# Seven-product feed-forward loop: products grown in two PSUM chains, partial sums copied out by ScalarE

## The chip, the cores and the metric

One core of a Trainium2 chip runs the whole network in one launch. The metric is device time in microseconds (us). Engines: TensorE (PE; its weight loads are PEld), VectorE (DVE), ScalarE (ACT), GpSimd (POOL) and SyncE (SP), which issues most DMAs. TensorE writes to PSUM, which has eight banks; VectorE and ScalarE read it.

## The reference

Two layers with Macaron feed-forward blocks over 512 latent and 256 context tokens, width 1024, hidden width 2816, all in float32. A feed-forward block is

```
def swiglu(h, w_in, w_out):
    a, b = jnp.split(h @ w_in, 2, axis=-1)
    return (jax.nn.silu(a) * b) @ w_out

def ffn_substep(x, mods, w_in, w_out, g, b):
    shift, scale, gate = mods
    y = swiglu(modulate(x, shift, scale), w_in, w_out)
    return layer_norm(ALPHA * x + MACARON * gate * y, g, b)
```

It stands four times in the program, twice in each layer: FF1 and FF2 around the even mixer of layer 0, FF3 and FF4 around the odd one of layer 1. FF1 to FF3 work on 768 tokens, FF4 on the 512 latent ones. The modulation (`mods`) of each substep is a product of the conditions with `w_ada`.

## The kernel before

Features lie on partitions. Every float32 operand is split into a high and a low float32r part: ScalarE casts the high part (line 115), VectorE subtracts it for the low part (line 117), and a product is three matmuls, high by high, high by low, low by high (`mm3`, lines 154 to 156).

The hidden layer (`ffn`) has 22 blocks of 128 hidden units, each with gate weights (A1 = A11, A12) and value weights (A2 = A21, A22). The first 3 blocks (5 in FF4) are plain products. The other 19 (17) go through `seven`: the 2 x 2 products over halves of features and halves of tokens (384 columns each, 256 in FF4) are made of seven products in Winograd's form, each 4 steps of three matmuls, 84 matmuls in a block. They are named here in the order in which TensorE runs them: P1 = A11 B11, P2 = A12 B21, P3 = S2 T2, P4 = S1 T1, P5 = S3 T3, P6 = S4 B22, P7 = A22 T4. T1 to T4 are made once (tiles `six` and `xh`), S1 to S4 for each block. In the text a prime marks what belongs to the next block.

Around one block x, other engines do this:

- GpSimd makes the next blocks' S1, S2, S3 from freshly loaded weights (lines 645, 646, 647: **sum 1, sum 2, sum 3**; `ahead`) and S4' (line 654).
- ScalarE and VectorE split A1', S12', A2' and S4' (tiles `r4h`, `r4l`, `r4s`, eight buffers, seven used in a block). A1' has the number of its raw weights in its name; S12' is read from `late`, S4' goes to `r4s`.
- Raw weights come by DMA into four buffers `raw`, two in a block; the second load for block x+2 waits until S4 of block x is split.
- Each product has a PSUM bank of its own out of seven (`ps`, tag h). P1 is copied out by ScalarE (line 670), and VectorE adds the others to copies in SBUF: seven additions a block (line 668). Two silu run on ScalarE (672, 679). `put` multiplies gate and value (556, 560); what belongs to the second half of the tokens goes to DRAM.
- In FF1 and FF2 the **modulation** of later substeps runs beside the first 13 of the 19 blocks (`ada`): 24 loads of `w_ada`, for each one VectorE product with running sum for the latent tokens (line 183) and one for the context tokens, which by turns is a second one on VectorE, or a product on GpSimd (line 186) that ScalarE then sums (line 187). FF3 has 16 such loads, latent only; FF4 has none.

Each engine runs its instructions in one order, which a scheduler fixes when the program is built. Names in the rows end in a buffer's number.

Of the kernel before, what the change touches and what calls it, by code (L numbers as in the profile page):

```python
# [14 lines left out]
AF = mybir.ActivationFunctionType  # L15
# [3 lines left out]
P = 128  # L19
D = 1024  # L20
# [21 lines left out]
class Net:  # L42
# [70 lines left out]
    def split(self, h, l, src, lo="vector"):  # L113
        """src = h + l, each in float32r"""
        self.copied = self.nc.scalar.copy(out=h, in_=src)  # L115
        eng = self.nc.vector if lo == "vector" else self.nc.gpsimd
        eng.tensor_sub(out=l, in0=src, in1=h.bitcast(F32))  # L117

    def weights(self, dram, lo="vector", spare=None):
        """spare: a pool with room for them beside the stream's"""  # L120
# [10 lines left out]
    def behind_weights(self):  # L131
        """for loads and copies that would else be queued before those of the last weights"""
        st = ExitStack()
        for i in self.fetched:
            st.enter_context(self.tc.issue_after(i.ins))
        return st

    def late(self):
        """for what a phase leaves to the next: the second half's norm works there"""
# [11 lines left out]
    def mm3(self, ps, h, l, xh, xl, first, last):  # L151
        """first, last: of the products that go to the bank, in which two sums may lie"""
        mm = self.nc.tensor.matmul
# [5 lines left out]
    def load_c(self, tiles):  # L159
        """silu of the conditions in every partition; the first call leaves it in DRAM for the later ones"""  # L160
# [38 lines left out]
    def ada(self, sections, tiles, room, steps):  # L199
        """the modulation's sections, (layer, section), in so many steps; tiles for the conditions, room() for weights: [P, D]"""  # L200
# [24 lines left out]
    def start(self, pool):  # L225
        """The first modulation, half of the features after the other; yields before the first block and after each.
        The modulation's columns are made on the tensor engine, which has nothing else to do yet."""
# [47 lines left out]
    def affine(self, l, i, nxt):  # L275
        """columns of the norm's affine and, with the next modulation folded in, of the next input"""
# [68 lines left out]
    def rsqrt(self, a, eps_tile, eps, y, t):  # L345
        """y = 1/sqrt(a + eps): exp(-ln/2), then one step of Newton"""
# [9 lines left out]
    def table(self, name, after):  # L356
        """a function table ahead of its use; the one with both exp and ln the scheduler would else fetch apart"""
# [4 lines left out]
    def out_phase(self, pool, nk, wsrc, gsplit, halves, gate, l, i, nxt, r_of, table=None, keep=False, ada=iter(())):  # L362
        """y^T = w^T g over nk blocks; gsplit(kk, c0, c1) -> (hi, lo) of blocks 2kk, 2kk+1;
        wsrc(q, kk) -> [P, 1024] of blocks 2kk, 2kk+1 and the features' half q"""
# [11 lines left out]
        def operands(step):  # L376
            """the second pass loads the weights again, and ahead to where the first half's operand was,
            unless there is room to keep them"""
# [66 lines left out]
    def add_up(self, s, r, j):  # L445
        """the blocks' sum in two parts, of the even and the odd"""
# [19 lines left out]
    def settle(self, steps=None):  # L466
        """what is left of the norm of the second half: its first steps, or all"""
# [4 lines left out]
    def project(self, ws, halves, ps_of, done, group, early=None, spare=None, after=None):  # L472
        """ws: list of weight APs; ps_of(u, h) -> PSUM AP for half h (None: both in one), done(u, h) once it is there.
        The first `group` weights go half by half, and the second half of the input may come late;
        with `early`, which makes the input, they go block by block."""
# [54 lines left out]
    def ffn(self, l, p, halves, nxt, ada=((), ()), table=None, first_of_all=False):  # L530
        """ada: what else is to be made of the conditions while the hidden layer's two products go on"""
# [6 lines left out]
        with ExitStack() as st:  # L538
# [13 lines left out]
            def put(x, a, b, gate, up):  # L552
                """the hidden layer's block x, tokens a..b; the first half's stay on chip"""
# [11 lines left out]
            def r_of(h, j):  # L565
                """sums of the output product and the residual; the first half's later blocks lie where G was"""
# [13 lines left out]
            def ps_of(u, h):  # L580
                """a narrow half's gate and value share a bank"""
# [23 lines left out]
            # tokens in two halves of m, as in the seven products of Strassen and Winograd  # L605
# [5 lines left out]
            def sums_of_inputs():  # L611
                """T2 = B22 - T1, T3 = B22 - B12, T4 = B21 - T2 of T1 = B12 - B11"""
# [23 lines left out]
            def ahead(x, sums):  # L636
                """block x of the gate's weights, A11 and A12, and of the value's, A21 and A22: the sums but one,
                S1 = A21 + A22, S2 = S1 - A11, S3 = A11 - A21 (in A21's place)"""
# [11 lines left out]
            def seven(x, raw, sums):  # L650
# [10 lines left out]
                def product(w, b):  # L661
                    ps = self.ps()[:, :m]
                    for k in range(4):
                        ks = slice(k * P, (k + 1) * P)
                        self.mm3(ps, w[0][:, ks], w[1][:, ks], b[0][:, k, :], b[1][:, k, :], k == 0, k == 3)
                    return ps

                add = lambda o, a, b: nc.vector.tensor_add(out=o, in0=a, in1=b)  # L668
                u2, c11, u4, c22 = (self.tmp("c")[:, :m] for _ in range(4))
                nc.scalar.copy(out=u2, in_=product(part(A1, 0), B(0, 0)))  # L670
                add(c11, u2, product(part(A1, 1), B(1, 0)))
                nc.scalar.activation(out=c11, in_=c11, func=AF.Silu)
                add(u2, u2, product(part(S12, 1), made[2]))
# [646 lines left out]
```

## Time and profile before

| | us |
|---|---|
| median of 3 runs (lowest to highest) | 2876.92 (2876.66 to 2877.67) |
| span of the profiled execution | 2874.1 |
| TensorE busy | 2685.2 (93%) |
| VectorE busy | 2185.1 (76%) |
| ScalarE busy | 1237.0 (43%) |
| GpSimd busy | 1074.6 (37%) |

The profiled execution has no time of its own beside its span; the median is 2.8 us above it, which is what lies around the span. Busy shares are means over stages with different limits; the loop of each feed-forward block has to be read by itself.

### The profile page before, as it was taken

The page shows a single profiled execution, that of the slowest core. Times are in us where ns is not written, and L with a number is a line of the kernel's source. Part 1 is how long each engine was busy: PE and PEld are TensorE (multiplying, and loading weights), DVE is VectorE, ACT ScalarE, POOL GpSimd, SP SyncE. Part 2 cuts the span into 40 slices and gives each one's busy share as a digit, 9 for nine tenths or more (in the row PEclk, how much of TensorE's full clock was granted, in tenths as well). Part 3 has the DMA queues.
Part 4 walks back from the last instruction along what each step waited for, and adds up shares of the span by engine and source line. Part 5 has one row for each costly group of instructions (what it writes and reads, how often), then busy time and mean ns, then how long its engine had stood idle before and what let it go on. Part 6 is the DMA issues. An engine that isn't in the chain of part 4 may idle for free.

```text
span 2874.1 us, 44394 instructions
## 1 busy us (share of the span) xinstructions
PE 2685.2 (93%) x17168; PEld 2449.1 (85%) x17168; DVE 2185.1 (76%) x3131; ACT 1237.0 (43%) x1919; POOL 1074.6 (37%) x762
## 2 busy tenths in 40 slices
PE   7889999999999888999999899999999998999997
PEld 4789998887877778989788899998987777999997
DVE  3999978765774689997977888664745887778856
ACT  2333333544543343333345433332534667544444
POOL 0655522241220465643334644410424332366402
PEclk9999999999999999999999999999999999999998
DMA  5343255542114223334555333254541101423454
GB/s 221 111 147 112 105 174 207 195 152 67 56 37 152 88 96 139 118 119 139 206 200 180 110 134 119 82 189 165 184 149 59 41 34 45 158 92 122 155 192 157
DMA packets 139671, 374.24 MB, mean 130 GB/s; under 512 B 16962, under 2 KB 48066, under 8 KB 139460
## 3 DMA queue, kind: packets, MB, share of 16 engines
q1 hardware_dynamic: 136832, 370.21, 37.3%
q8 instruction: 135, 2.21, 0.3%
q10 hardware_dynamic: 2628, 1.20, 0.2%
q14 instruction: 76, 0.62, 0.1%
HBM read 337.78 MB, written 33.56 MB: 129 GB/s over the span
## 4 chain that ended last, share of the span: by engine, by line
PE 58%; DVE 22%; issue 7%; ACT 5%; POOL 4%; DMA 3%; SPq 0%; DVEq 0%; POOLq 0%; ACTq 0%
PE ps L156 17%; PE ps L154 17%; PE ps L155 17%; DVE r4l L117 3%; DVE trash L183 3%; DVE c L668 2%; DVE spare L556 1%; DMA raw<-in_w_ffn_out 1%; PE ps L1187 1%; PE ps L1188 1%; PE ps L1189 1%; DVE sm L1089 1%; DVE b L621 1%; ACT r4h L115 1%; DVE late_g L560 1%
## 5 line engine op out<-in xcount | busy, mean ns | idle before, releaser
L117 DVE TENSOR_TENSOR r4l<-raw,r4h 128x1024 fp32r<-128x1024 f32 (+1 forms) x350 | 449.5, 1286 | 215.5 <-ACT r4h L115 176.3
L154 PE MATMUL ps<-xh,r4h 128*128 128x384 f32 (+2 forms) x1672 | 562.5, 337 | 16.6 <-ACT xh L115 7.0
L155 PE MATMUL ps<-xl,r4h 128*128 128x384 f32 (+2 forms) x1672 | 559.1, 335 | 4.8 <-DVE xl L117 3.2
L156 PE MATMUL ps<-xh,r4l 128*128 128x384 f32 (+2 forms) x1672 | 559.0, 335 | 0.0
L115 ACT CAST r4h<-raw 128x1024 fp32r<-128x1024 f32 (+1 forms) x366 | 358.7, 982 | 443.2 <-PE ps L155 330.7
L156 PE MATMUL ps<-six,r4l 128*128 128x384 f32 (+1 forms) x888 | 294.7, 332 | 69.5 <-DVE r4l L117 69.5
L154 PEld LDWEIGHTS ps<-xh,r4h 128*128 128x128 f32 x1672 | 315.1, 189 | 39.7 <-ACT xh L115 9.5
L155 PEld LDWEIGHTS ps<-xl,r4h 128*128 128x128 f32 x1672 | 315.4, 189 | 24.8 <-DVE xl L117 4.9
L156 PEld LDWEIGHTS ps<-xh,r4l 128*128 128x128 f32 x1672 | 315.4, 189 | 18.1
L668 DVE TENSOR_TENSOR c<-c,ps 128x384 f32<-128x384 f32 (+1 forms) x518 | 261.8, 518 | 49.4 <-PE ps L156 39.5
L154 PE MATMUL ps<-six,r4h 128*128 128x384 f32 (+1 forms) x888 | 292.6, 330 | 0.0
L155 PE MATMUL ps<-six,r4h 128*128 128x384 f32 (+1 forms) x888 | 291.4, 328 | 0.0
L156 PE MATMUL ps<-r4h,r4l 128*128 128x512 f32 (+1 forms) x768 | 278.5, 363 | 13.7 <-DVE r4l L117 13.7
L154 PE MATMUL ps<-r4h 128*128 128x512 f32 (+1 forms) x768 | 278.6, 363 | 0.0
L155 PE MATMUL ps<-r4l,r4h 128*128 128x512 f32 (+1 forms) x768 | 277.3, 361 | 0.0
L156 PE MATMUL ps<-r4h,spare 128*128 128x256 f32 (+1 forms) x896 | 261.0, 292 | 11.5 <-DVE spare L117 11.5
L154 PE MATMUL ps<-r4h,spare 128*128 128x256 f32 (+1 forms) x896 | 263.6, 294 | 1.5 <-ACT spare L115 1.5
L155 PE MATMUL ps<-r4l,spare 128*128 128x256 f32 (+1 forms) x896 | 260.6, 291 | 0.1
L156 PEld LDWEIGHTS ps<-six,r4l 128*128 128x128 f32 x888 | 170.8, 192 | 77.6 <-DVE r4l L117 77.6
L645 POOL TENSOR_TENSOR late<-raw 128x512 f32<-128x512 f32 x74 | 116.6, 1575 | 255.1 <-DMA raw<-in_w_ffn_in 219.2
L654 POOL TENSOR_TENSOR raw<-raw,late 128x512 f32<-128x512 f32 x74 | 98.2, 1327 | 251.3 <-DVE r4l L117 233.8
L156 PEld LDWEIGHTS ps<-r4h,spare 128*128 128x128 f32 x896 | 172.8, 193 | 16.3 <-DVE spare L117 14.2
(292 smaller groups left out, 5969.8 us busy)
## 6 DMA issues: line engine op xcount, KB each, us to landing
raw<-in_w_ffn_in SPq DMA_DIRECT2D x176, 512.0 KB, 4.0
raw<-in_w_ffn_out SPq DMA_DIRECT2D x176, 512.0 KB, 4.2
spare<-in_w_ada SPq DMA_DIRECT2D x80, 512.0 KB, 5.0
six<-in_w_ada SPq DMA_DIRECT2D x64, 512.0 KB, 5.3
g<-late_g SPq DMA_DIRECT2D x88, 128.0 KB, 2.2
raw<-g SPq DMA_DIRECT2D x44, 256.0 KB, 3.3
raw<-in_w_in_even SPq DMA_DIRECT2D x20, 512.0 KB, 3.4
raw<-in_w_in_odd SPq DMA_DIRECT2D x16, 512.0 KB, 3.3
```

Of the source, the lines that this page charges most:

```text
L115: self.copied = self.nc.scalar.copy(out=h, in_=src)
L117: eng.tensor_sub(out=l, in0=src, in1=h.bitcast(F32))
L154: mm(out=ps, lhsT=h, rhs=xh, start=first, stop=False)
L155: mm(out=ps, lhsT=h, rhs=xl, start=False, stop=False)
L156: mm(out=ps, lhsT=l, rhs=xh, start=False, stop=last)
L183: nc.vector.scalar_tensor_tensor(out=self.tmp("trash").bitcast(BF16), in0=r, scalar=1.0, in1=self.c_bc[v], op0=ALU.mult, op1=ALU.mult, acc ...
L556: nc.vector.tensor_mul(out=G(x)[:, 0, a:e], in0=gate[:, :e - a], in1=up[:, :e - a])
L560: nc.vector.tensor_mul(out=t, in0=gate[:, o:b - a], in1=up[:, o:b - a])
L621: sub = lambda o, a, b: nc.vector.tensor_sub(out=o, in0=a, in1=b)
L645: nc.gpsimd.tensor_add(out=s1, in0=a21, in1=a22)
L654: nc.gpsimd.tensor_sub(out=a12, in0=a12, in1=sums[:, 512:])
L668: add = lambda o, a, b: nc.vector.tensor_add(out=o, in0=a, in1=b)
```

## The change

In `seven` the products no longer have a bank each. X takes P1, then P3, P5 and P7 on top; Y takes P4, then P6. P2 keeps its own. Sums on the way are read between two products of a chain: ScalarE copies X after P1 (u1) and after P3 (u2), and Y after P4 (p5); VectorE adds P2 to u1, X after P5 to p5, and Y after P6 to u2. X after P7 goes straight into `put`. The flag `chain` only tells the builder that a bank is read inside a group. (The diff also drops comments, so lines move by one to ten.)

```
-                def product(w, b):
-                    ps = self.ps()[:, :m]
+                def grow(ps, w, b):
+                    first = ps is None
+                    ps = self.ps()[:, :m] if first else ps
                     for k in range(4):
                         ks = slice(k * P, (k + 1) * P)
-                        self.mm3(ps, w[0][:, ks], w[1][:, ks], b[0][:, k, :], b[1][:, k, :], k == 0, k == 3)
+                        self.mm3(ps, w[0][:, ks], w[1][:, ks], b[0][:, k, :], b[1][:, k, :], first and k == 0, k == 3,
+                                 True)
                     return ps
 
                 add = lambda o, a, b: nc.vector.tensor_add(out=o, in0=a, in1=b)
-                u2, c11, u4, c22 = (self.tmp("c")[:, :m] for _ in range(4))
-                nc.scalar.copy(out=u2, in_=product(part(A1, 0), B(0, 0)))
-                add(c11, u2, product(part(A1, 1), B(1, 0)))
-                nc.scalar.activation(out=c11, in_=c11, func=AF.Silu)
-                add(u2, u2, product(part(S12, 1), made[2]))
-                add(u4, u2, product(part(S12, 0), made[1]))
-                p7 = product(part(A2, 0), made[3])
-                add(c22, u4, p7)
-                add(u2, u2, p7)
-                add(u4, u4, product(S4, B(1, 1)))
-                nc.scalar.activation(out=u4, in_=u4, func=AF.Silu)
-                add(u2, u2, product(part(A2, 1), made[4]))
-                put(x, 0, m, c11, u2)
-                put(x, m, n, u4, c22)
+                copy = lambda o, a: nc.scalar.copy(out=o, in_=a)
+                u1, u2, p5 = (self.tmp("c")[:, :m] for _ in range(3))
+                X = grow(None, part(A1, 0), B(0, 0))
+                copy(u1, X)
+                add(u1, u1, grow(None, part(A1, 1), B(1, 0)))
+                nc.scalar.activation(out=u1, in_=u1, func=AF.Silu)
+                grow(X, part(S12, 1), made[2])
+                copy(u2, X)
+                Y = grow(None, part(S12, 0), made[1])
+                copy(p5, Y)
+                grow(X, part(A2, 0), made[3])
+                add(p5, p5, X)
+                grow(Y, S4, B(1, 1))
+                add(u2, u2, Y)
+                nc.scalar.activation(out=u2, in_=u2, func=AF.Silu)
+                grow(X, part(A2, 1), made[4])
+                put(x, 0, m, u1, X)
+                put(x, m, n, u2, p5)
```

TensorE's instructions stand in the same order as before. On the other engines the order moves in all four loops. ScalarE, late in FF1's modulation, before (one block's tail and the next one's head; `spare` with `mod` is the sum of line 187):

```order
L679 ACTIVATE c_1751<-c_1751 128x384
L670 COPY c_1895<-ps_1899 128x384
L115 CAST r4s_1892<-raw_1726 128x512
L187 ACTIVATE spare_1720,mod_0_1_102<-spare_1720 128x1024
L115 CAST r4h_2026<-raw_1872 128x1024
L672 ACTIVATE c_1896<-c_1896 128x384
L115 CAST r4h_2030<-late_528 128x1024
```

And now, about the same place (c_1840 is u2, c_1841 p5, c_1979 the next block's u1):

```order
L675 COPY c_1840<-ps_1842 128x384
L675 COPY c_1841<-ps_1884 128x384
L116 CAST r4h_1972<-raw_1818 128x1024
L689 ACTIVATE c_1840<-c_1840 128x384
L189 ACTIVATE spare_1810,mod_0_1_102<-spare_1810 128x1024
L116 CAST r4s_1976<-raw_1816 128x512
L116 CAST r4h_2102<-raw_1956 128x1024
L675 COPY c_1979<-ps_1982 128x384
```

The modulation's sum stood behind the copy of P1 and the cast of S4'; now it stands ahead of both casts and of the copy. In the blocks before these (the second to the seventh of the loop) it stands one place further up, ahead of the second silu. VectorE at this place, before, from the additions of P5 on (`trash` is the modulation's product, r4l_1889 the low part of A2'):

```order
L668 TENSOR_TENSOR c_1752<-c_1751,ps_1810 128x384
L668 TENSOR_TENSOR c_1749<-c_1749,ps_1810 128x384
L183 SCALAR_TENSOR_TENSOR trash_1862,mod_0_0_101<-spare_1581,spare_697 128x1024
L668 TENSOR_TENSOR c_1751<-c_1751,ps_1825 128x384
L183 SCALAR_TENSOR_TENSOR trash_1864,mod_0_1_102<-spare_1581,spare_698 128x1024
L556 TENSOR_TENSOR spare_1854<-c_1751,c_1752 128x128
L560 TENSOR_TENSOR late_g_1857<-c_1751,c_1752 128x256
L668 TENSOR_TENSOR c_1749<-c_1749,ps_1840 128x384
L183 SCALAR_TENSOR_TENSOR trash_1868,mod_0_0_101<-spare_1720,spare_697 128x1024
L556 TENSOR_TENSOR spare_1854<-c_1750,c_1749 128x384
L117 TENSOR_TENSOR r4l_1889<-raw_1728,r4h_1888 128x1024
L117 TENSOR_TENSOR r4s_1892<-raw_1726,r4s_1892 128x512
```

And now, from the low part of A1' on:

```order
L118 TENSOR_TENSOR r4l_1964<-raw_1816,r4h_1963 128x1024
L674 TENSOR_TENSOR c_1839<-c_1839,ps_1856 128x384
L118 TENSOR_TENSOR r4l_1968<-late_528,r4h_1967 128x1024
L185 SCALAR_TENSOR_TENSOR trash_1944,mod_0_0_101<-spare_1804,spare_697 128x1024
L674 TENSOR_TENSOR c_1841<-c_1841,ps_1842 128x384
L185 SCALAR_TENSOR_TENSOR trash_1946,mod_0_1_102<-spare_1804,spare_698 128x1024
L195 TENSOR_TENSOR mod_0_0_101<-mod_0_0_101,bada_86 128x8
L185 SCALAR_TENSOR_TENSOR trash_1952,mod_0_0_101<-spare_1810,spare_697 128x1024
L674 TENSOR_TENSOR c_1840<-c_1840,ps_1884 128x384
```

One modulation product now stands between the low part of S12' and the addition for which P7 waits (c_1841). The product on `spare_1810`, on which GpSimd's product and then ScalarE's sum hang, is the third of the block.

## Rows read from the trace of the kernel before

**Rows 1.** The page of the whole execution: its span, and part 1 (busy time, share of the span, instructions, by engine; PEld is TensorE's weight loads).

```profile
span 2874.1 us, 44394 instructions
PE 2685.2 (93%) x17168; PEld 2449.1 (85%) x17168; DVE 2185.1 (76%) x3131; ACT 1237.0 (43%) x1919; POOL 1074.6 (37%) x762
```

**Rows 2.** Busy time of each engine in six stretches of the seven-product loops: FF1 while the modulation runs beside it, and after; FF2 likewise; FF3; FF4. Columns: stretch and its length, then busy us and number of instructions of TensorE, its weight loads, VectorE, ScalarE and GpSimd, granted clock, DMA share, GB/s.

```profile
106.00:302.40 196.40, 177.95 (x979) 174.78 (x978) 192.55 (x234) 71.92 (x108) 103.92 (x56) 0.98 0.38 134
302.40:410.00 107.60, 106.06 (x597) 104.79 (x596) 84.48 (x124) 38.21 (x53) 42.91 (x26) 1.00 0.35 117
1057.00:1252.00 195.00, 178.24 (x976) 174.84 (x976) 191.37 (x234) 69.86 (x106) 104.26 (x56) 0.98 0.38 135
1252.00:1361.00 109.00, 107.08 (x602) 105.73 (x601) 87.28 (x127) 38.08 (x53) 43.66 (x26) 1.00 0.34 117
1643.60:1910.00 266.40, 266.40 (x1511) 265.97 (x1510) 201.37 (x289) 92.67 (x125) 109.41 (x68) 1.00 0.35 119
2565.90:2727.00 161.10, 161.10 (x1347) 161.10 (x1347) 141.97 (x211) 76.60 (x112) 88.05 (x57) 1.00 0.40 134
```

**Rows 3.** The copy of the first product (line 670, one in each hidden block) in each of the four loops: count, ns min/median/max, start of the first and of the last one.

```profile
L670 ACT COPY c<-ps x19: 458/467/480, 106.0 to 395.8; 128x384 f32<-128x384 f32 x19
L670 ACT COPY c<-ps x19: 457/462/479, 1057.0 to 1346.3; 128x384 f32<-128x384 f32 x19
L670 ACT COPY c<-ps x19: 469/479/481, 1631.3 to 1895.2; 128x384 f32<-128x384 f32 x19
L670 ACT COPY c<-ps x17: 361/373/374, 2553.2 to 2716.9; 128x256 f32<-128x256 f32 x17
```

**Rows 4.** What TensorE waited for in FF1's loop (106 to 410 us, first row) and in FF2's (1057 to 1361 us): us in total, times, longest.

```profile
PE ps L156 <- DVE r4l L117: 19.2, 11, 2.9
PE ps L156 <- DVE r4l L117: 17.8, 11, 2.9
```

**Rows 5.** Lines 668, 117, 183, 186 and 654 in FF1's loop beside the modulation (106 to 302.4 us): count, ns min/median/max, start of the first and last, shape.

```profile
L668 DVE TENSOR_TENSOR c<-c,ps x82: 539/546/556, 109.0 to 302.0; 128x384 f32<-128x384 f32 x82
L117 DVE TENSOR_TENSOR r4l<-raw,r4h x24: 1211/1215/3414, 107.3 to 297.2; 128x1024 fp32r<-128x1024 f32 x24
L117 DVE TENSOR_TENSOR r4s<-raw,r4s x12: 677/680/2879, 108.4 to 296.1; 128x512 fp32r<-128x512 f32 x12
L117 DVE TENSOR_TENSOR r4l<-late,r4h x12: 1225/1764/2141, 112.3 to 298.8; 128x1024 fp32r<-128x1024 f32 x12
L183 DVE SCALAR_TENSOR_TENSOR trash<-spare x31: 1212/1835/3225, 114.4 to 291.1; 128x1024 bf16<-128x1024 f32 x31
L183 DVE DVE_READ_ACCUMULATOR trash<-spare x31: 76/77/84, 115.5 to 292.2; 128x1 f32 x31
L186 POOL TENSOR_TENSOR spare<-spare x11: 2391/2583/3383, 115.7 to 292.4; 128x1024 f32<-128x1024 f32 x11
L654 POOL TENSOR_TENSOR raw<-raw,late x12: 1283/1292/1317, 110.8 to 298.6; 128x512 f32<-128x512 f32 x12
```

**Rows 6.** The timeline of GpSimd and VectorE in FF1 (start and length in us; the wait ahead of it in brackets): one place where they meet.

```profile
239.61 2.62 POOL L186 TENSOR_TENSOR spare<-spare 128x1024 f32<-128x1024 f32 x1 [3.32 <-DVE trash L183]
239.93 3.38 DVE L117 TENSOR_TENSOR r4l<-raw,r4h 128x1024 fp32r<-128x1024 f32 x1
```

**Rows 7.** ScalarE's timeline in FF1 (columns as above).

```profile
236.44 0.62 ACT L115 CAST r4s<-raw 128x512 fp32r<-128x512 f32 x1
242.26 1.06 ACT L187 ACTIVATE spare<-spare 128x1024 f32<-128x1024 f32 x1 [5.20 <-POOL spare L186]
243.22 0.18 ACT L187 ACTIVATION_READ_ACCUMULATOR spare<-spare 128x1 f32 x1
243.32 1.03 ACT L115 CAST r4h<-raw 128x1024 fp32r<-128x1024 f32 x1
244.41 0.52 ACT L672 ACTIVATE c<-c 128x384 f32<-128x384 f32 x1
```

**Rows 8.** The timeline of one hidden block of FF3: the first matmul of the third, the fifth and the seventh product, VectorE's two subtractions (rows in order of engine, not of time).

```profile
1749.07 0.34 PE L154 MATMUL ps<-six,r4h 128*128 128x384 f32 x1
1753.30 0.34 PE L154 MATMUL ps<-six,r4h 128*128 128x384 f32 x1
1757.52 0.34 PE L154 MATMUL ps<-six,r4h 128*128 128x384 f32 x1
1749.15 1.23 DVE L117 TENSOR_TENSOR r4l<-raw,r4h 128x1024 fp32r<-128x1024 f32 x1 [1.26 <-issue]
1753.39 1.23 DVE L117 TENSOR_TENSOR r4l<-late,r4h 128x1024 fp32r<-128x1024 f32 x1 [1.46 <-PE ps L155]
```

**Rows 9.** One weight load of FF1: the subtraction that frees its buffer, its issue on SyncE's queue, and GpSimd's first sum from it.

```profile
226.89 0.69 DVE L117 TENSOR_TENSOR r4s<-raw,r4s 128x512 fp32r<-128x512 f32 x1 [1.39 <-ACT r4s L115]
227.61 0.33 SPq L642 DMA_DIRECT2D raw<-in_w_ffn_in  x1
230.94 1.74 POOL L645 TENSOR_TENSOR late<-raw 128x512 f32<-128x512 f32 x1 [0.49 <-DMA raw<-in_w_ffn_in]
```

**Rows 10.** Busy time and granted clock in two stretches of FF1 (columns as in rows 2).

```profile
240.00:243.40 3.40, 0.83 (x6) 0.51 (x4) 3.40 (x3) 1.14 (x3) 2.23 (x1) 1.00 0.74 263
243.60:246.90 3.30, 3.30 (x11) 3.30 (x11) 3.29 (x5) 3.15 (x4) 1.15 (x1) 0.50 0.76 232
```

**Rows 11.** Line 668 in FF4's loop (columns as in rows 5).

```profile
L668 DVE TENSOR_TENSOR c<-c,ps x112: 405/415/423, 2568.4 to 2725.5; 128x256 f32<-128x256 f32 x112
```

More of the change, by code (lines that the diff above doesn't have):

```diff
@@ L1 @@
+import functools
 import itertools
@@ L149, in ps, with mm3 @@
         return self.psum.tile([P, 512], F32, tag=tag, name="ps", bufs=self.psum_bufs[tag])
-    def mm3(self, ps, h, l, xh, xl, first, last):
-        mm = self.nc.tensor.matmul
+    def mm3(self, ps, h, l, xh, xl, first, last, chain=False):
+        mm = functools.partial(self.nc.tensor.matmul, skip_group_check=chain)
         mm(out=ps, lhsT=h, rhs=xh, start=first, stop=False)
```

## Prediction

> **What bounds the kernel now.** I read the page first, then the loops one by one. TensorE is busy 93% of the span, no other engine over 76% [rows 1], so only a stage in which TensorE waits can give anything. The stretches show where it does in the loops that change: in FF3 and FF4 it is busy for the whole stretch, 266.4 of 266.4 us and 161.1 of 161.1, while in FF1 and FF2, as long as the modulation runs beside them, it lacks 18.5 and 16.8 us, and after that less than 2 [rows 2]. A block at full pace takes 14.79 us: four products lie between 1749.07 and 1757.52, 2.113 us each, times seven [rows 8]. From the first copy to the last, 18 blocks, FF1 takes 289.8 us and FF2 289.3 [rows 3], against 266.2 at full pace: they lose 23.6 and 23.1 us, **46.7 in all, the most that the change can win in the loops**. What TensorE waits for there is, 11 times in each loop and up to 2.9 us, a low part of weights from VectorE [rows 4]. VectorE is busy for 192.6 of those 196.4 us [rows 2]. The first 13 blocks bear the loss, so a block there takes about 14.79 + 23.4/13 = 16.6 us.
>
> That VectorE is full does not mean that it works all the time. An addition from PSUM takes 0.54 to 0.56 us throughout; a subtraction of two SBUF operands takes 1.21 us at best and up to 3.41 [rows 5]. One such stands beside GpSimd's product: it starts at 239.93, the product ends at 242.23, the subtraction at 243.31, 1.08 later [rows 6]. The two take turns.
>
> The Trainium skill has this as a rule ("SBUF — State Buffer", section "Who interferes with whom"): a VectorE instruction with two SBUF inputs and a GpSimd instruction that reads SBUF exclude each other for a whole instruction; one with a single SBUF input goes free. The rows agree [rows 5, 6]. By the rule, the additions that go are of the free kind and made no one wait; rival B below is what that would mean here.
>
> **What the change removes.** Four of seven additions a block: 0.546 us each, less about 0.08 by which neighbours overlap, so 1.9 us of VectorE a block in FF1 to FF3, and 4 x 0.33 = 1.3 in FF4 (0.415 each [rows 11], same overlap). The large multiplication of `put` now reads PSUM; priced as the addition that is its nearest row, 0.55, it costs the same, but no longer takes turns with GpSimd. In FF3 and FF4 none of this is worth anything, since TensorE waits for nobody there.
>
> **What it adds.** Two copies a block on ScalarE, 0.47 us each [rows 3]. ScalarE is busy 71.9 of 196.4 us [rows 2], so its time is no matter; its order is. Before, each product had its own bank, and additions could run most of a block late. Now P3 may not start before u1 is copied, P5 not before u2, P6 not before p5, P7 not before VectorE has added X to p5; between each sum and its reader's deadline lies one product, 2.1 us (1.4 in FF4). Whatever stands ahead of these four in its queue, TensorE now waits for.
>
> *P3 and the modulation's sum.* ScalarE's sum (line 187) waits for GpSimd's product: ScalarE stood idle for 5.20 us before one of them [rows 7]. So far the copy of P1 mostly went first. Now, as the order shows, both casts and u1's copy for the next block stand behind it, and the product hangs, in the later blocks, on the third modulation product. That closes a loop, from one start of P3 to the next:
> - P3 and P4 until S12' can be split: 4.32 [rows 8]; the subtraction, 1.23 [rows 8]
> - three modulation products with their read-outs, 3 x (1.21 + 0.08) = 3.87 [rows 5], and the addition to p5, 0.55 [rows 5]
> - GpSimd's product, 2.58 [rows 5]; ScalarE's sum, 1.06 + 0.18; the casts of S4' and of the next A1, 0.62 and 1.03 [rows 7]; u1's copy, 0.47 [rows 3]
>
> That is 15.9 us; eight neighbours on one engine overlap by 0.09, so 15.2. GpSimd's three sums for the block after next must fit in as well. Their weights land 3.3 us after the load, which follows the split of S4' [rows 9], so one sum finishes before the subtraction of S12' and two take turns with VectorE's instructions: 2 x 1.29 [rows 5], of which the free addition hides 0.5. About 17.2 us.
>
> In the earlier blocks the sum stands before the second silu, and GpSimd's product follows the first modulation product, so the loop is 4.32 + 1.23 + 1.29 + 2.58 + 2 x 1.29 (the other modulation products) + 0.55 + 0.52 (silu [rows 7]) + 0.62 + 1.03 + 0.47 = 15.2, less 0.7, and again two sums, 2.58: 17.1, or a little under. I take 17.0 for both; bounds are 15.2 with all three sums out of the way and 18 with all three in it. Eleven of the 13 blocks have three modulation products and lose 17.0 - 14.8 = 2.2 us each; the two lighter ones and the loop's start some 2 together: 26 us, against 23.4 now. **FF1 and FF2: +2.8 each, +5.6.**
>
> *P7 in FF3.* Thirteen blocks have one modulation product between the subtraction of S12' and the addition to p5. From P3's start: 4.32 + 1.23 + 1.29 + 0.55, less 0.2, is 7.2; P7 is due at 8.45 [rows 8]. With one of GpSimd's sums between, 8.5: even. With two, up to 9.8: 1.4 late. A1' is split until 1.31 after P3's start [rows 8], GpSimd makes S4' until 2.6, and then its sums as their weights land; I take one and a part, 0.4 us a block, between nothing and 1.4. **FF3: +5.2 (0 to 18).**
>
> *FF4* has no modulation: S12' can be split two products after P3 starts, 2.9 (161.1 us for 1347 matmuls, times 12, is 1.435 a product [rows 2]); with the subtraction, one sum of GpSimd between, and the addition (0.42 [rows 11]), 5.7, when P7 is due (4 x 1.435). **0 (to 1.3 in each of 16 blocks).** Ahead of u2's copy ScalarE has the cast of S12', long done. The other waits (P5 for u2 with the first silu ahead of it, P6 for p5) have a microsecond to spare outside the modulation, and lie within the loop in it.
>
> **Sum.** 5.6 + 5.2 + 0 = +10.8. The profiled execution has a span of 2874.1 us and the median is 2876.92, so 2.8 us lie around it and stay. 2876.9 + 10.8 = **2888 us**, slower by 0.4%; by its own terms 2876 to 2906. About 0.2%, 5.8 us, is what a measurement of this kernel can tell from no change.
>
> **The rivals.**
> - *A: VectorE was the bound, and it is relieved (faster).* Twelve blocks have 12 x 1.9 = 23 us fewer in 192.6, 14.2 a block, under TensorE's 14.79 [rows 2]. If u1's copy then comes in time, each block loses perhaps 0.6: 2 x (23.4 - 13 x 0.6) = -31, **2846**; with nothing lost, 2830. For it: VectorE has no idle time there now. Against it: it now has to wait inside each block, for four readings in turn. It decides at a loop of 16.7 us: below that FF1 and FF2 gain, 2.2 us for each 0.1.
> - *B: the turns with GpSimd are the bound.* A full block has three subtractions of 1.21, one of 0.68, three products of 1.21, and GpSimd's 4 x 1.29 + 2.58 [rows 5]: 15.7 us that exclude each other, with `put` above 16, near the 16.6 found. Of this only the large multiplication leaves, 0.55 in 22 blocks: -12, and FF3's +5: **2870**.
> - *C: gaps also cost clock.* After a gap of 2.6 us (TensorE busy 0.83 of 3.40) the granted clock was 0.50, the 1.2 GHz level, for 3.3 us [rows 10], which costs 1.7. If half of the 22 full blocks have such a gap at P3, 19 more: **2907**.
>
> **Chances.** Forecast 0.40 (of which 0.07 within 0.2%), A 0.25, B 0.19 (0.08 faster by over 0.2%, 0.11 within), C 0.16. Faster 0.33, same 0.18, slower 0.49. The range, 2848 to 2912, leaves out the best half of A and the worst part of C, and the far ends of FF3 and FF4.
>
> **What would show it.** In FF1 and FF2, TensorE's wait for low parts should give way to waits at P3 for the copy of u1, ScalarE's longest wait should still be the one for GpSimd's product, and the time from copy to copy should be near 17 us for 13 blocks. In FF3, small waits at P7 for the addition to p5, in 13 blocks. VectorE's busy time should fall by about 74 x 1.8 = 130 us without a gain. I am wrong if the first copy to the last takes less than 285 us in FF1; wrong in FF3 if it stays at 263.9.

## The result, and the profile after

The changed kernel takes 2917.68 us (median; 2914.74 to 2918.6) against 2877.3 of the kernel before in the same runs: ratio 1.0137, interval 1.0122 to 1.0152. It is slower, as forecast, by 40 us where 11 were forecast and the range ended at 2912. The page of its profiled execution, span and part 1:

```profile
span 2913.0 us, 43903 instructions
PE 2706.1 (93%) x17168; PEld 2464.9 (85%) x17168; DVE 2027.2 (70%) x2835; ACT 1294.9 (44%) x2067; POOL 1094.0 (38%) x762
```

VectorE has 158 us less to do than in [rows 1], and the span is 39 us longer. Where they arise is read by one mark in every loop, the first silu (once in each block, line 672 before, 680 after). Count, ns, start of the first and of the last one, for FF1 to FF4, before:

```profile
L672 ACT ACTIVATE c<-c x19: 506/526/528, 109.7 to 399.4; 128x384 f32<-128x384 f32 x19
L672 ACT ACTIVATE c<-c x19: 508/526/529, 1061.9 to 1350.0; 128x384 f32<-128x384 f32 x19
L672 ACT ACTIVATE c<-c x19: 524/526/527, 1636.1 to 1898.9; 128x384 f32<-128x384 f32 x19
L672 ACT ACTIVATE c<-c x17: 417/419/422, 2556.1 to 2719.3; 128x256 f32<-128x256 f32 x17
```

and after:

```profile
L680 ACT ACTIVATE c<-c x19: 522/525/527, 108.5 to 415.8; 128x384 f32<-128x384 f32 x19
L680 ACT ACTIVATE c<-c x19: 523/525/528, 1078.8 to 1380.9; 128x384 f32<-128x384 f32 x19
L680 ACT ACTIVATE c<-c x19: 524/525/528, 1666.2 to 1937.3; 128x384 f32<-128x384 f32 x19
L680 ACT ACTIVATE c<-c x17: 418/420/422, 2595.5 to 2757.4; 128x256 f32<-128x256 f32 x17
```

FF1 has grown from 289.7 to 307.3 us, FF2 from 288.1 to 302.1, FF3 from 262.8 to 271.1; FF4 has gone from 163.2 to 161.9. Together +38.6, nearly all of the span's growth (38.9). The same stretches as in [rows 2] (FF1 beside the modulation, FF2 beside it, FF3):

```profile
106.00:302.40 196.40, 176.29 (x924) 172.43 (x922) 154.66 (x180) 74.74 (x119) 110.31 (x55) 0.93 0.36 127
1074.00:1269.00 195.00, 174.20 (x924) 170.46 (x924) 156.60 (x181) 73.65 (x120) 109.01 (x55) 0.94 0.36 128
1676.60:1942.90 266.30, 262.85 (x1483) 260.29 (x1482) 162.13 (x204) 106.62 (x159) 108.53 (x67) 1.00 0.32 110
```

VectorE, full before, now idles for 42 of 196 us, and TensorE does fewer matmuls in the same time (924 for 979), in part at 1.2 GHz (granted clock 0.93 on the mean). What TensorE waits for, in FF1 (120 to 420 us), FF2 (1085 to 1400) and FF3 (1676 to 1960): us in total, times, longest.

```profile
PE ps L156 <- ACT c L675: 24.9, 10, 4.8
PE ps L156 <- ACT c L675: 24.2, 11, 4.8
PE ps L156 <- DVE c L674: 4.6, 7, 1.1
```

The wait for a low part of weights [rows 4] is gone; in its place stands ScalarE's copy of u1, for which P3 waits, and in FF3 the addition to p5, for which P7 waits. One such place in FF1, from GpSimd's product of the modulation to P3 and on (start, length, in brackets the wait ahead):

```profile
243.32 3.34 POOL L188 TENSOR_TENSOR spare<-spare 128x1024 f32<-128x1024 f32 x1
246.70 1.06 ACT L189 ACTIVATE spare<-spare 128x1024 f32<-128x1024 f32 x1 [3.45 <-POOL spare L188]
247.75 0.60 ACT L116 CAST r4s<-raw 128x512 fp32r<-128x512 f32 x1
248.26 1.04 ACT L116 CAST r4h<-raw 128x1024 fp32r<-128x1024 f32 x1
248.63 0.88 SPq L644 DMA_DIRECT2D raw<-in_w_ffn_in  x2
249.21 0.47 ACT L675 COPY c<-ps 128x384 f32<-128x384 f32 x1
249.73 0.69 PE L156 MATMUL ps<-six,r4h 128*128 128x384 f32 x1 [4.80 <-ACT c L675]
256.28 1.29 POOL L647 TENSOR_TENSOR late<-raw 128x512 f32<-128x512 f32 x1 [4.28 <-DMA raw<-in_w_ffn_in]
256.97 1.68 DVE L118 TENSOR_TENSOR r4l<-late,r4h 128x1024 fp32r<-128x1024 f32 x1 [5.95 <-PE ps L157]
258.57 2.31 DVE L185 SCALAR_TENSOR_TENSOR trash<-spare 128x1024 bf16<-128x1024 f32 x1
264.41 2.40 POOL L188 TENSOR_TENSOR spare<-spare 128x1024 f32<-128x1024 f32 x1 [2.39 <-DVE trash L185]
269.87 0.44 PE L156 MATMUL ps<-six,r4h 128*128 128x384 f32 x1 [1.87 <-ACT c L675]
```

This is the loop of the prediction, in its order: the product ends, ScalarE sums it, casts S4' and the next A1, copies u1, and P3 starts, 3.1 us after the product. But it takes 20.1 us here, not 17.0. The first matmul after the wait takes 0.69 us, S12' is split 7.2 us after P3's start instead of 4.3, and GpSimd's first sum starts 7.1 us after the later of its block's two loads was issued instead of 3.3 [rows 9]. Not every block takes this path to P3; those that do not are told with the step that failed.

### The profile page after: what moved, and what is told of

It is laid out like the page before. It is cut to its first block, busy times and chain, and to the rows that moved or that the text cites. A ratio compares the mean times of both kernels' runs of the same rounds, so it can differ in the third digit from the quotient of the medians.

```text
span 2913.0 us, 43903 instructions
## 1 busy us (share of the span) xinstructions
PE 2706.1 (93%) x17168; PEld 2464.9 (85%) x17168; DVE 2027.2 (70%) x2835; ACT 1294.9 (44%) x2067; POOL 1094.0 (38%) x762
## 4 chain that ended last, share of the span: by engine, by line
PE 62%; DVE 16%; POOL 7%; issue 6%; ACT 5%; DMA 3%; SPq 0%; DVEq 0%; POOLq 0%; ACTq 0%
PE ps L156 18%; PE ps L157 18%; PE ps L158 18%; DVE r4l L118 2%; DVE trash L185 2%; POOL spare L188 1%; DMA raw<-in_w_ffn_out 1%; PE ps L1197 1%; PE ps L1198 1%; PE ps L1199 1%; DVE sm L1099 1%; DVE b L623 1%; ACT r4h L116 1%; POOL raw L649 1%; POOL late L648 1%
## 5 line engine op out<-in xcount | busy, mean ns | idle before, releaser
L118 DVE TENSOR_TENSOR r4l<-raw,r4h 128x1024 fp32r<-128x1024 f32 (+1 forms) x350 | 438.9, 1255 | 249.7 <-ACT r4h L116 176.4
L156 PE MATMUL ps<-xh,r4h 128*128 128x384 f32 (+2 forms) x1672 | 566.1, 340 | 12.6 <-DVE K L1044 6.7
L156 PE MATMUL ps<-six,r4h 128*128 128x384 f32 (+1 forms) x888 | 302.1, 340 | 95.8 <-ACT c L675 89.1
L157 PE MATMUL ps<-six,r4h 128*128 128x384 f32 (+1 forms) x888 | 296.7, 334 | 0.0
L158 PE MATMUL ps<-r4h,r4l 128*128 128x512 f32 (+1 forms) x768 | 277.8, 362 | 12.6 <-DVE r4l L118 12.4
L156 PEld LDWEIGHTS ps<-six,r4h 128*128 128x128 f32 x888 | 173.4, 195 | 109.2 <-ACT c L675 97.5
L118 DVE TENSOR_TENSOR r4l<-late,r4h 128x1024 fp32r<-128x1024 f32 x74 | 111.1, 1502 | 171.2 <-PE ps L157 167.4
L158 PEld LDWEIGHTS ps<-r4h,spare 128*128 128x128 f32 x896 | 173.5, 194 | 20.1 <-DVE spare L118 17.9
```

The source lines that it names most:

```text
L156: mm(out=ps, lhsT=h, rhs=xh, start=first, stop=False)
L157: mm(out=ps, lhsT=h, rhs=xl, start=False, stop=False)
L158: mm(out=ps, lhsT=l, rhs=xh, start=False, stop=last)
```

## The experiments

All ratios are to the kernel before in the same runs. FF1, FF2 and FF3 are from the first silu to the last, in us.

| kernel | ratio (interval) | FF1 | FF2 | FF3 |
|---|---|---|---|---|
| before | 1 | 289.7 | 288.1 | 262.8 |
| changed | 1.0137 (1.0122 to 1.0152) | 307.3 | 302.1 | 271.1 |
| e1_fill | 1.0214 (1.0197 to 1.0231) | 311.5 | 315.1 | 269.9 |
| e2_sumtwice | 1.0176 (1.0161 to 1.0191) | 313.6 | 311.2 | 271.4 |
| e3_sumlate | 0.9906 (0.9891 to 0.9920) | 273.9 | 273.2 | 271.8 |
| e4_allvec | 0.9800 (0.9784 to 0.9815) | 268.4 | 266.8 | 271.0 |
| e5_before_sumlate | 0.9967 (0.9954 to 0.9980) | 285.1 | 284.6 | 262.9 |
| e6_before_allvec | 0.9848 (0.9833 to 0.9863) | 279.8 | 279.4 | 263.4 |
| e7_sttlate | 1.0122 (1.0106 to 1.0139) | 307.4 | 304.9 | 266.0 |
| e8_allvec_sttlate | 0.9786 (0.9771 to 0.9801) | 270.5 | 267.6 | 266.3 |
| e9_fill4 | 1.0125 (1.0108 to 1.0142) | 304.8 | 300.7 | 270.3 |
| e10_nosum3 | 1.0042 (1.0027 to 1.0057) | 293.6 | 293.7 | 270.2 |
| e11_before_nosum3 | 0.9907 (0.9893 to 0.9922) | 279.7 | 277.8 | 263.1 |
| e12_s4first | 1.0088 (1.0068 to 1.0107) | 298.7 | 296.2 | 271.6 |

### Is it the place of ScalarE's sum?

```
 ... (in ada_block)
-                nc.scalar.activation(out=r, in_=r, func=AF.Copy, accum_out=col(v))
+                self.later(lambda c=col(v): nc.scalar.activation(out=r, in_=r, func=AF.Copy, accum_out=c))
 ... (in seven)
-                copy(p5, Y)
+                first = copy(p5, Y)
+                with tc.issue_after(first.ins):
+                    self.pay()
```

> The changed kernel, with ScalarE's sum of the modulation put behind the next block's copy of Y after P4 (p5), so that no copy that TensorE waits for stands behind it. Theory 1 (the order on ScalarE made the loss in FF1 and FF2): waits at P3 for u1's copy all but vanish, so do most stretches at 0.50; what is left is the turns of VectorE and GpSimd, some 16.4 us a full block: FF1 from first to last copy 285 to 291 us (307.2 in the changed kernel, 289.8 before), the whole 2880 to 2890 us. Rival A (four additions fewer are worth their 1.9 us once the order is out of the way): 14.9 to 15.5 us a block, FF1 270 to 277, the whole 2850 to 2862. Rival (VectorE's own chain is as long without ScalarE): no change, 2914 to 2920.

FF1 falls by 33 us to 273.9, the whole from 1.0137 to 0.9906: the sum moved in ScalarE's queue turns 1.4% slower into 0.9% faster. (The small instructions that end a section of the modulation wait with it on VectorE, and a few rows of VectorE near it changed places.) TensorE's waits for u1's copy shrink to this in FF1, FF2 is alike (columns as above; the line is 685 here):

```profile
PE ps L156 <- ACT c L685: 3.8, 7, 0.8
```

So the sum's place accounts for the whole loss in FF1 and FF2, and for more: with it out of the way the loops are shorter than before. The gain is larger than my theory's: it is what rival A gave, 15.4 us a block.

To see whether the chains had a part in that gain, the same move was made without them, behind the first silu:

> The kernel before, with ScalarE's sum of the modulation put behind the next block's first silu: the same move as in e3_sumlate, without the chains. It tells whether the 15.4 us a block found there come from the move alone or from the four additions that the chains save. Theory 1 (before, VectorE's own work set the pace, the sum stood in nobody's way; the chains do relieve VectorE once the order lets them): FF1 stays at 286 to 291 us (289.8 before), the time within 0.3% of the kernel before. Rival (the sum's place alone is worth it, in either kernel): FF1 272 to 277 us, 1 to 1.3% faster.

285.1: 4.6 us from the move alone. With the chains 273.9, so these are worth 11 us a loop, as soon as the order lets them.

### The modulation's products all on VectorE

```
-            if v == LAT or j % 2:
+            if True:
```

> The changed kernel, with all of the modulation's products on VectorE (24 more of 1.21 us in all where GpSimd had 24 of 2.58 and ScalarE 24 sums). VectorE gets 0.9 products a block more and takes turns with 2.58 us less of GpSimd's. Theory 1 with the turns: neither ScalarE's sum nor GpSimd's product is in the loop; a block has 4.3 us of subtractions, 3.7 x 1.21 of products, 4 x 1.29 of GpSimd's sums, 0.7 of the product from SBUF that exclude each other: 14.7, just under TensorE's 14.8: a block takes 14.9 to 15.6 us, FF1 270 to 278, the whole 2850 to 2866 us. Rival (VectorE is the bound by its busy time or its order): 16.5 us or more a block, FF1 289 or more, the whole 2880 or more.

> The kernel before, with all of the modulation's products on VectorE, as in e4_allvec without the chains. By the turns alone (theory B) a block has 14.7 us of work that excludes each other and 0.55 more of the large multiplication: 15.3, FF1 272 to 277 us, 1% faster than before. By VectorE's busy time (theory A): 192.6 us in 12 blocks and 12 x 0.9 x 1.29 = 14 more make 17.2 a block: FF1 296 us or more, slower than before. With e4_allvec at 268.3 the difference is what four additions are worth here.

With the chains, FF1 runs at 268.4, TensorE's own pace but for 2 us: VectorE's queue has room for the added products. TensorE's waits for u1's copy, 24.9 us in the changed kernel, are 0.7 us in FF1 (120 to 420 us). Without the chains 279.8 is reached, between the two expectations: 15.8 us a block is more than the work that takes turns (15.3) and far less than the 17.2 of busy time. In the 13 blocks the chains save 11.4 us (12.6 in FF2), 0.9 us a block of the 1.9 that four additions take. Not all of this need be the additions': the chains also take `put`'s large multiplication out of the turns, which the forecast's rival B prices at 0.55 a block, and no run separates the two. And since FF1 is 2 us from TensorE's own pace with the chains, 11.4 is the least that they give VectorE here.

### Longer and shorter in the same queue

The sum done twice:

```
-                nc.scalar.activation(out=r, in_=r, func=AF.Copy, accum_out=col(v))
+                for _ in range(2):
+                    nc.scalar.activation(out=r, in_=r, func=AF.Copy, accum_out=col(v))
```

> The changed kernel, with ScalarE's sum of the modulation done twice over (same result), 1.24 us more of ScalarE's time in each of 24 sums. ScalarE is busy 38% there. Theory 1 (the sum stands in the loop from P3 to P3): each of the 22 to 24 blocks with a sum grows by 1.2 us, more where the clock falls too, FF1 from 307 to 321 us or a little more, the whole 2944 to 2960 us. Rival B (VectorE's and GpSimd's turns set the pace, ScalarE has room): no change, 2914 to 2920.

+6.3 and +9.1 us, half of what theory 1 asks and not the nothing of rival B. The trace shows where the other half went: in the later blocks the scheduler put u1's copy ahead of the cast of A1 when it placed the second sum, so there only 1.24 - 1.04 came on top, and they take as long as in the changed kernel. The second to the seventh block grew, by 0.7 us each in FF1 and 1.5 in FF2. In FF1 the sum is on the path to P3 only in every other one of these: from P3 to P3 those take 20.5, 19.3 and 20.4 us (19.1, 18.1 and 18.1 in the changed kernel), and the ones between, where it is not, 17.3, 17.7 and 16.9 (18.1, 17.1 and 17.6).

The other way round, the sum one place later, behind the cast of S4' alone (as e3_sumlate, with the last lines behind `self.split(*S4, a12)`):

> The changed kernel, with ScalarE's sum of the modulation one or two places later: behind the cast of S4', still ahead of the cast of the next A1 and of u1's copy, for which P3 waits. GpSimd's and SyncE's orders stay, TensorE's too. Theory 2 in full (the loop that sets 18 us does not run through TensorE: ScalarE's sum, the cast of S4' behind it, its subtraction, the load that takes its buffer, GpSimd's three sums, GpSimd's product, ScalarE's sum again): the split of S4' and the load come free of the sum, that loop is open, and what is left is the one through P3, forecast at 17.0 less the cast's 0.6: 16.4 a block in 12 blocks, FF1 from first to last copy 288 to 294 us (307.2 in the changed kernel), the whole 26 to 40 us shorter, ratio 1.000 to 1.005. Rival (the loop through P3 alone makes the 18): only the cast's 0.6 us a block, FF1 299 to 302, ratio 1.008 to 1.010.

-8.6 and -5.9 us: about the 0.6 of the cast in each block, which is the rival's price. Opening the loop that goes through the load and not through TensorE brought nothing beyond that, so it does not set the pace by itself. Time on ScalarE between GpSimd's product and u1's copy counts in full in the blocks where that path ends last (e2_sumtwice); here it is 0.7 us a block in FF1 and 0.5 in FF2 for the cast's 0.6.

### Is it the clock?

```
+                if l == 0 and x < plain + 13:
+                    grow(None, part(A1, 1), B(1, 0))
                 grow(X, part(S12, 1), made[2])
```

> The changed kernel, with twelve more matmuls (P2 once more, into a bank that nobody reads) ahead of P3 in the first 13 blocks of FF1 and FF2: 26 x 2.11 = 55 us more work for TensorE. Theory 1 (the wait at P3 lowers the granted clock, P3 and P4 then run at 1.2 GHz, and they lie inside the loop from P3 to P3, so the gap feeds itself): the added work fills the gap, the granted clock stays at 1.00 in most blocks, P3 to the split of S12' takes 4.3 us instead of up to 7.2, and a block takes 17.0 to 17.3 us although TensorE has 16.9 to do; FF1 from first to last copy 292 to 299 us (307.2 in the changed kernel), the whole 2890 to 2902 us. Theory 2 (the loop is 18 us by its own terms, the clock falls in time that is idle anyway): nothing is gained, 307 us or more in FF1, the whole 2915 to 2925. Theory 3 (TensorE's own time counts): 55 us more, 2970.

The clock did what theory 1 says, the time did not: 0.99 granted in the same stretch of FF1, and 311.5 us. The result is not clean, since the added matmuls also made the scheduler move rows on VectorE, ScalarE and GpSimd. So the same with nine matmuls in four blocks, which moves neighbours, and in one block of each loop GpSimd's product from behind its first sum to behind all three:

> The changed kernel, with nine more matmuls (1.58 us, into a bank that nobody reads) ahead of P3 in four blocks of FF1 and of FF2 alone: the third, fifth, seventh and ninth of the loop, where FF1 waited 3.8, 3.0, 3.1 and 4.8 us at P3 and ran at 0.50 afterwards. Unlike in e1_fill the other engines keep their order but for a few neighbours. Theory 1 (the low clock lies in the loop): 27 of 32 us at 0.50 go in FF1, worth 13, and the gaps shrink with them: FF1 from first to last copy 292 to 298 us (307.2 in the changed kernel), the whole 10 to 20 us shorter, ratio to before 1.006 to 1.010. Theory 2 (GpSimd's queue is as long: its sums and then the product that ScalarE's sum waits for end no sooner): the clock stays up, and the time doesn't move, FF1 303 to 309, ratio 1.012 to 1.015.

FF1's stretch beside the modulation in e1_fill and in e9_fill4 (columns as in [rows 2]):

```profile
106.00:302.40 196.40, 185.02 (x1021) 181.26 (x1020) 144.36 (x175) 73.80 (x118) 104.58 (x53) 0.99 0.36 125
106.00:302.40 196.40, 177.42 (x956) 173.87 (x954) 144.47 (x180) 75.42 (x122) 107.71 (x55) 0.96 0.37 129
```

The mean clock rises from 0.93 to 0.96 in FF1, so by the mean less than half of the slow time went, and FF1 gains 2.5 us, FF2 1.4; the whole, 1.0125, stays within the interval of the changed kernel. The changed kernel says more without an experiment. Its stretches from one start of P3 to the next, in FF1 from the second block on:

```profile
121.95:141.03 19.08, 15.20 (x86) 14.55 (x85) 14.43 (x19) 6.82 (x12) 11.96 (x6) 0.97 0.26 89
141.03:159.16 18.13, 17.62 (x84) 17.30 (x84) 12.41 (x14) 6.88 (x12) 9.82 (x5) 0.84 0.39 147
159.16:177.22 18.06, 15.02 (x84) 14.68 (x84) 15.62 (x21) 6.66 (x12) 10.90 (x6) 1.00 0.28 95
177.22:194.30 17.08, 16.61 (x84) 16.28 (x84) 13.48 (x18) 6.89 (x12) 9.61 (x5) 0.90 0.44 162
194.30:212.38 18.08, 15.03 (x85) 14.68 (x85) 16.57 (x20) 6.67 (x12) 11.04 (x6) 0.98 0.28 102
212.38:229.98 17.60, 17.60 (x84) 17.55 (x85) 10.82 (x12) 6.72 (x11) 9.29 (x5) 0.83 0.41 150
229.98:249.73 19.75, 14.95 (x86) 14.61 (x85) 15.92 (x18) 6.93 (x12) 11.28 (x5) 0.98 0.26 83
249.73:269.87 20.14, 18.08 (x85) 17.43 (x85) 14.19 (x19) 6.88 (x12) 9.35 (x5) 0.85 0.36 130
269.87:287.50 17.63, 15.33 (x84) 14.68 (x84) 14.48 (x17) 6.88 (x12) 9.36 (x5) 1.00 0.23 83
287.50:306.94 19.44, 15.05 (x85) 14.72 (x85) 14.62 (x17) 6.89 (x12) 10.38 (x5) 1.00 0.48 163
306.94:325.05 18.11, 16.84 (x85) 16.20 (x85) 13.41 (x17) 6.90 (x12) 8.49 (x5) 0.91 0.19 57
```

The five with a longer stretch at 1.2 GHz (clock 0.83 to 0.91) take 18.2 us on the mean, the other six (0.97 to 1.00) 18.7. So it does not take the low clock to make 18 us. It is not free either. The block at 177.22 and the next one have their like in FF2, with GpSimd's work in the same order, where the first of the two runs at full clock:

```profile
1144.74:1160.26 15.52, 15.04 (x84) 14.72 (x85) 13.48 (x18) 6.77 (x12) 8.89 (x5) 1.00 0.48 178
1160.26:1178.35 18.09, 15.04 (x84) 14.71 (x85) 16.55 (x20) 6.66 (x12) 10.77 (x6) 0.98 0.29 101
```

It takes 1.6 us less, and the next block does not give this back. What the low clock costs over a whole loop is not shown: e1_fill and e9_fill4 both moved other rows as well.

### What GpSimd's sums cost in the loop

```
-                nc.gpsimd.tensor_sub(out=a21, in0=a11, in1=a21)
+                if l or not plain < x < plain + 13:
+                    nc.gpsimd.tensor_sub(out=a21, in0=a11, in1=a21)
```

> The changed kernel, with GpSimd's third sum left out in 12 blocks of FF1 and of FF2 (S3 is then not A11 - A21 but A21); the order of everything else stays. The sum takes 2.19 us on average in the changed kernel beside the modulation, 1.29 undisturbed. Theory 2 (the loop from P3 to P3 runs through GpSimd's three sums and the product behind them): a block falls by 1.3 to 2.2 us, FF1 from 307.2 to 281 to 291 us, the whole 32 to 50 us shorter, ratio 0.997 to 1.003. Theory 1 (the loop runs through P3 and P4 at the low clock and VectorE's products): VectorE waits once less for its turn, at most 0.9 a block, FF1 296 to 305.

> The kernel before with the same sum left out: what it is worth without the chains. By the turns (theory B) the pace of before is the sum of the work that excludes each other, and 1.29 us less of it a block make FF1 273 to 277 us (289.8 before). If VectorE's own queue sets the pace, it wins only the part of the turns that it waits for: 280 to 287.

The changed kernel gains 13.7 us in FF1 and 8.4 in FF2, 0.9 a block: between the two theories. The kernel before gains 10.0 and 10.3, as much: so the sums are in the way in both kernels alike, and this pair doesn't tell what the chains add. In the changed kernel nothing else moved, and with two sums left a full block (the second to the twelfth, from first silu to first silu) takes 17.0 us on the mean in either loop, where it took 18.3 in FF1 and 17.9 in FF2 with three.

### FF3

```
-                add(p5, p5, X)
+                self.last_add = add(p5, p5, X)
 ...
-                next(ada, None)
+                with tc.issue_after(self.last_add.ins) if l else nullcontext():
+                    next(ada, None)
```

> The changed kernel, with the modulation's product in FF3 (13 blocks) put behind the addition of X to p5, for which P7 waits; FF1 and FF2 as they are. Theory 1 (P7 is late by what stands between S12' and that addition): FF3 from first to last copy falls from 272.1 to 264 to 267 us, the waits at P7 go, 5 to 8 us in all, ratio to before 1.011 to 1.013 (1.0137 for the changed kernel). Rival (GpSimd's sums make the addition late, or the loss is that of the first blocks): 270 to 272 us, no change.

FF3 falls from 271.1 to 266.0, and TensorE waits for nothing between 1684 and 1942 us. That is 5.1 us; FF3's other 3.2 stay, nearly all in its first block (below).

> The changed kernel with both moves: all modulation products on VectorE (e4_allvec, ratio 0.980) and FF3's product behind the addition to p5. If the two stages are apart, FF1 and FF2 as in e4_allvec (268 us each) and FF3 as in e7_sttlate (264 to 267): ratio 0.977 to 0.979. In FF1 and FF2 nothing is moved.

2823.78 us against 2883.55, ratio 0.9786: FF1 to FF3 at 270.5, 267.6 and 266.3. Of the kernels tried this is the fastest, 3.5% faster than the changed kernel by two moves of the modulation; its interval overlaps that of e4_allvec. The Trainium skill ("Perfetto Trace Analysis", section "Optimizing Tensor Performance") would have independent matmul groups rotate through PSUM banks, so that one is read while the next is written. The chains keep to this, since every product follows one on another bank; and a bank that is read between two products of its chain costs TensorE nothing (no wait in FF3 between 1684 and 1942 us of e7_sttlate), as long as nothing late stands ahead of the readers.

## Why the prediction was wrong in size

- **What bounds the kernel, and what takes its place: right.** The wait for low parts gave way to P3's wait for u1's copy, behind the modulation's sum; ScalarE's longest wait is still for GpSimd's product (9.8 us in FF1). That the sum's place makes the loss is shown by e3_sumlate.
- **The loop of 17.0 us: mis-sized, 18.3.** This is the step that failed. Of FF1 and FF2 together +5.6 was forecast, and +31.6 measured; eleven full blocks in each, at 18.3 us in FF1 and 17.9 in FF2 instead of 17.0, make some 23 of the 26 us between. The term is that of GpSimd's sums, of which the working had two in the loop: "their weights land 3.3 us after the load", from one load [rows 9], so that one sum would be done before S12' is split. In FF1 eight of the eleven blocks have all three sums ahead of GpSimd's product, and in only one of these (at 306.94, where S12' is late at the low clock) has a sum ended before the subtraction of S12' starts. With two sums left the loop does take 17.0 (e10_nosum3). The loads of this line beside the modulation in FF1, after, from issue to landing (smallest, median, largest; the trace has 16 landings of 23 loads):

```profile
DMA to landing us min/median/max: 3.1/5.9/8.5
```

  The same line in the kernel before has a median of 5.5, up to 8.1: the row that I took was among the shortest, and the trace had the others. They go with what was issued just ahead: of the 16, four come more than 4 us after the last other weight load and land in 3.1 to 3.5 us, as the one of [rows 9] does; the eight that have two or more others in the 3 us before them take 5.9 to 8.5.

  In the block at 287.50 (19.4 us at full clock) the load is issued with P3, the sums start 7.2 us later, behind the subtraction of S12' (291.93), and GpSimd's product, behind them in its queue, starts at 301.50, 14.0 after P3, where the forecast's terms come to 11.6 (4.32 + 1.23 + 3.87 + 0.55 and two turns, less the overlaps). In the block at 269.87 the first sum starts 4.1 after P3, and the block takes 17.6. So 18, "with all three in it", was the better centre. That an earlier landing would bring the loop to 17.0 was not tried.

  In the earlier blocks the path was wrong as well. GpSimd's product was to follow the first modulation product; in every other one it stands behind the three sums in GpSimd's own queue, and P3 waits for all of them. The block that starts at 159.16 (18.06 us, clock 1.00):

```profile
161.99 1.29 POOL L656 TENSOR_TENSOR raw<-raw,late 128x512 f32<-128x512 f32 x1 [2.36 <-DVE r4l L118]
164.52 1.42 POOL L647 TENSOR_TENSOR late<-raw 128x512 f32<-128x512 f32 x1 [1.24 <-DMA raw<-in_w_ffn_in]
166.02 2.15 POOL L648 TENSOR_TENSOR late<-late,raw 128x512 f32<-128x512 f32 x1
168.13 2.27 POOL L649 TENSOR_TENSOR raw<-raw 128x512 f32<-128x512 f32 x1
170.38 3.37 POOL L188 TENSOR_TENSOR spare<-spare 128x1024 f32<-128x1024 f32 x1
173.78 1.06 ACT L189 ACTIVATE spare<-spare 128x1024 f32<-128x1024 f32 x1 [8.69 <-POOL spare L188]
```

- **The modulation products and sums at their undisturbed price.** In this stretch the product on VectorE takes 1.97 us on the mean (1.21 in the sum), GpSimd's sums 1.71, 2.12 and 2.19 (1.29):

```profile
L185 DVE SCALAR_TENSOR_TENSOR trash<-spare 128x1024 bf16<-128x1024 f32 x31 | 60.6, 1973 | 0.5 <-ACT c L675 0.5
L649 POOL TENSOR_TENSOR raw<-raw 128x512 f32<-128x512 f32 x11 | 24.0, 2185 | 0.0
L648 POOL TENSOR_TENSOR late<-late,raw 128x512 f32<-128x512 f32 x11 | 23.3, 2122 | 0.7
L647 POOL TENSOR_TENSOR late<-raw 128x512 f32<-128x512 f32 x11 | 18.8, 1711 | 29.2 <-DMA raw<-in_w_ffn_in 29.2
```

  The working had two turns for it; with three sums behind S12' there are three. VectorE's busy time fell by 158 us all the same, where 130 were forecast.
- **FF3, +5.2: right as far as it goes** (5.1 of the 8.3, removed by e7_sttlate), with P7 as the place; that the 0.4 a block, set between nothing and 1.4, came out so close is in part luck. What was missed is the start of the loops. P3 of the first block waits for u1's copy, which on ScalarE stands behind the casts of T1 to T4. In FF1 (88 to 108 us), before and after:

```profile
PE ps L156 <- DVE r4l L117: 10.7, 1, 10.7
PE ps L156 <- ACT c L675: 13.4, 1, 13.4
```

  2.7 us, and as much in FF2 (12.5 and 15.2); in FF3 the first block's two copies of P1 lie 15.2 us apart instead of 12.4.
- **FF4, nothing: right.** A block takes 10.2 us before and 10.1 after.
- **Rival C** came nearest to the number, 2907, but not by its mechanism: the stretches at 1.2 GHz are there (0.93 and 0.94 for 0.98), and one costs 1.6 us where it can be compared, yet the blocks without a longer one take 18.7 us on the mean, and e9_fill4, with less than half of the slow stretches gone, gained 2.5 us in FF1.
- **Rival A** was right about VectorE, and its condition failed: it decides at 16.7 us a block, and the loop took 18.3. With the sum out of the way 15.4 us came out.
- **Rival B**, beside which the rule of the Trainium skill stands ("SBUF — State Buffer", section "Who interferes with whom"), has the additions that go as free of cost. The chains' 11 us a loop (e3 against e5, e4 against e6) are about twice the 6 that this rival gives them, although the turns themselves are plain in the rows. That a free instruction still stands in the queue behind one that waits for its turn would explain it; no run shows this by itself.

## What to carry to other kernels

Where a change gives a reader a deadline, look at what stands ahead of it in its engine's queue, and first of all at what waits there for another engine: moving that one instruction was worth 2.3% here, more than the change itself could win or lose. Price the terms of such a loop by the median of all the rows in that stretch, not by a clean one: the load at 3.3 us and the product at 1.21 were the exceptions. And before a stretch at the low clock is counted as a loss, ask whether the path that ends last goes through TensorE there.

## What the runs showed of the hardware

- What a stretch at 1.2 GHz costs depends on the path: the changed kernel's blocks with one in FF1 (granted clock 0.83 to 0.91) took no longer on the mean (18.2 us) than the others (18.7 at 0.97 to 1.00), but two blocks with GpSimd's work in the same order took 17.08 us at 0.90 (FF1) and 15.52 at 1.00 (FF2).
- A 512 KB load of weights took 3.1 to 8.5 us to land in one and the same loop: 3.1 to 3.5 when no other weight load had been issued in the 4 us before it, 5.9 to 8.5 when two or more had been in the last 3 us.
- VectorE had room for 48 products of the modulation in each of the two loops instead of 36, as soon as GpSimd did without its own and ScalarE without its sums. TensorE was then busy 181.17 of 182 us in FF1 (e4_allvec):

```profile
120.00:302.00 182.00, 181.17 (x1024) 179.72 (x1023) 164.08 (x228) 71.68 (x111) 88.46 (x49) 1.00 0.40 139
```
